# Another order of work at the entry to a gated MLP: six first-half product pairs ahead, sums begun before the norm

## The chip, the cores and the metric

One core of one Trainium2 chip runs the whole program. The time is the device time in microseconds (us) of one execution. The engines of the core are TensorE (PE, with its weight loads shown apart as PEld), VectorE (DVE), ScalarE (ACT), GpSimd (POOL) and SyncE (SP), which here only starts DMA transfers.

## The reference, cut to what matters

One layer of a trunk over 1024 tokens of 1024 features, in fp32:

```python
mod = silu(c) @ ada_w + ada_b                    # 6 x 1024 values
sh1, sc1, g1, sh2, sc2, g2 = split(mod, 6)
h = modulate(rmsnorm(x), sh1, sc1)               # mixers: pooling and gated linear attention
y = concat([y_pool, y_gla]) @ w_out
x = x + g1 * y
h = modulate(rmsnorm(x), sh2, sc2)               # the MLP begins here
up = h @ w_up                                    # 1024 -> 2 x 2816
y = causal depthwise conv (width 3) of up, + conv_b
a, b = split(y, 2)
x = x + g2 * ((silu(a) * b) @ w_down)
return rmsnorm(x) * final_norm
```

`modulate(h, shift, scale)` is `h * (1 + scale) + shift`. The change lies at the line `h = modulate(rmsnorm(x), sh2, sc2)` and the first products of `h @ w_up`.

## The kernel before, in words

Activations lie feature by feature: a tile holds 128 features of 512 tokens, so there are two token halves (0 and 1) of eight tiles each. Every fp32 factor of a product is split into a rounded high part and the remainder (`wsplit`, `split_b`, `mod_split`: a cast on ACT, a subtraction on DVE), and each product is three matmuls (`mm3`: high by high, low by high, high by low).

The MLP's up-projection multiplies a 2x2 block of weights (two halves of the input features) with a 2x2 block of activations (two token halves) with seven products in place of eight, in the Strassen-Winograd manner. The seven kinds, for each of 22 output blocks i, are products of sums of weight blocks with sums of activation blocks. In the code (1, i) and (2, i) multiply blocks of token half 0 alone. Kinds 5, 6, 3, 7 and 4 need half 1: their activation operands `ops_a` are made by `norm2_second` from the eight tiles `x1[1]` of half 1, the eight normalised tiles `x1[0]` of half 0, and the row scale `r` of half 1. One product of one kind for one block is 12 matmuls (four tiles by three).

`order` is the list of products. The first RAMP = 3 blocks are a ramp: (1, i) and (2, i) of these come first, and (5, i), which needs half 1, follows; from block 3 on all seven kinds of a block stand together. `up_step` gives out one product: it accumulates in a PSUM bank, ACT copies results out (`sp`, `ca`, `u`) or back in as the start of another accumulation (`seeded`, tile `upy`; where the bank is among the first eight, one small matmul with `prime` or `w` goes ahead of the copy), DVE adds, and ACT and DVE do the convolution (`conv`). `up_weight` loads a 512 KB tile of `w_up` (tile `ua`, from the `raw` pool of four buffers), forms the weight sums on DVE and splits them into a buffer that `slot()` hands out (names `ws` and `xs`). `prepare(n)` does this ahead of need: LOOK = 4 products ahead.

Ahead of the MLP stand the mixers' projections (`r`, then `u` jobs), then `jobs_out(0)` and `jobs_out(1)`, the output projection for half 0 and half 1: eight jobs each, each with its own 512 KB tile of `w_out` (also in the `raw` pool), split into the `wh` and `wl` buffers, two of each. `evac` adds the gated result to x (L693, DVE), stores it, squares it on ACT, and POOL adds the squares (`nsa`); `rstd_of` sums over the features by a matmul with ones (`ss`) and takes the root with two ACT instructions (`nr`). The conditioning vector `mod` is made beside all this, one tile `ada` of 512 KB at a time (`mod_tile`, L216 and L219), again through the `raw` pool: `run_jobs(jobs, mods_each)` does `mods_each` such tiles after each job, 32 in all.

PE executes in the order in which the program gives it. On ACT, DVE, POOL and in SP's queue a planner moves instructions by its own estimates, and each then executes strictly in the order that it set.

Of the kernel before, what the change touches and what calls it, by code (L numbers as in the profile page):

```python
# [28 lines left out]
P = 128  # L29
NK = 8  # L30
S = 1024
T = 512
# [21 lines left out]
def trunk_kernel(ctx, tc, xT, cvec, adaT, vecs, w_start, w_z, w_qkru, w_v, w_g2, w_pool,  # L54
# [612 lines left out]
    def jobs_out(hf):  # L667
# [24 lines left out]
        def evac(d, pp):  # L692
            dve.scalar_tensor_tensor(out=x1[hf][d], in0=pp, scalar=modv[:, 16 + d:17 + d],  # L693
                                     in1=x1[hf][d], op0=ALU.mult, op1=ALU.add)
            nc.sync.dma_start(out=x1d[hf][d], in_=x1[hf][d])
            own = s2 if hf else None
            if d == 0:
                nacc[hf] = s2(name="nsa") if hf else tmp("nsa")
            nacc[hf] = sumsq_step(nacc[hf], d, x1[hf][d], pool_e, True, own)
        return [mk(i) for i in range(8)]  # L700

    nacc = {}
    x1d = [[tc.dram_tile([P, T], F32, name=f"x1d{hf}{d}") for d in range(NK)] for hf in range(2)]
    gd = [tc.dram_tile([P, S], F32, name=f"gd{m}") for m in range(NFF)]
# [56 lines left out]
    for names, mods_each in (("k0 z q0 k1 v0 v1 v2 v3 q1", 0), ("r0 r1 r2 r3", 2),  # L761
                             ("u0 u1 u2 u3", 1)):
        run_jobs([named[i] for i in names.split()], mods_each)
# [14 lines left out]
    def slot():  # L778
        tag = ("wh", "xs", "wl", "xs")[slot_n[0] % 4]
        slot_n[0] += 1  # L780
        if tag == "xs":
            t = xs_pool.tile([P, 2, 4, P], F32R, tag="xs", name="xs")
        else:
            t = wp.tile([P, 2, 4, P], F32R, tag=tag, name="ws")
        return t[:, 0], t[:, 1]
# [43 lines left out]

    RAMP = 3  # L830
    order = [(n, i) for i in range(RAMP) for n in (1, 2)]
    for i in range(NFF):
# [12 lines left out]

    prepare(2)
    run_jobs(late[5:], 1)
    php.close()
# [17 lines left out]
    def small(name):  # L866
        return up_pool.tile([P, T], F32, tag="u", name=name, bufs=6)

# [3 lines left out]
    def norm2_second():  # L872
        r = rstd_of(nacc[1], s2)
        shs = const.tile([P, 4], F32, name="shs")
        dve.tensor_tensor(out=shs, in0=modv[:, 24:28], in1=modv[:, 28:32], op=ALU.add)

        def a22(name, dt=F32):
            return up_pool.tile([P, T], dt, tag="a22", name=name, bufs=10)

        def split_b(t, bias, mk):  # L880
            h, l = mk(dt=F32R, name="sh"), mk(dt=F32R, name="sl")
            if bias is None:
                act.copy(out=h, in_=t)
                sub(dve, l, t, h.bitcast(F32))
            else:
                act.activation(out=h, in_=t, func=AF.Identity, bias=bias, scale=1.0)  # L886
                dve.scalar_tensor_tensor(out=l, in0=t, scalar=bias, in1=h.bitcast(F32),  # L887
                                         op0=ALU.add, op1=ALU.subtract)
            return h, l

        t0, t1 = x1
        sums = []
        for k in range(4):
            for kk in (k, k + 4):
                mod_head(t1[kk], t1[kk], r, 32, kk)
            s = a22("s1")
            dve.tensor_tensor(out=s, in0=t1[k], in1=t1[k + 4], op=ALU.add)
            ops_a[5][k] = split_b(s, shs[:, k:k + 1], s2)
            sums.append(s)
        for k in range(4):  # L900
            sub(pool_e, t1[k], t0[k], t1[k])
            sub(dve, sums[k], sums[k], t0[k])
            ops_a[6][k] = split_b(sums[k], modv[:, 28 + k:29 + k], s2)
        for k in range(4):
            sub(pool_e, t0[k + 4], t0[k + 4], sums[k])
            ops_a[3][k] = split_b(t0[k + 4], None, s2)
            ops_a[7][k] = split_b(t1[k], None, s2 if k < 3 else a22)
        for k in range(4):
            ops_a[4][k] = split_b(t1[k + 4], modv[:, 28 + k:29 + k], a22)

# [20 lines left out]

    def seeded(src, w):
        primed = banks[0] >= 8
        y = bank("upy")
        if not primed:
            mm(y, w[0][:, 0], ops_a[1][0][0], True, True)
        act.copy(out=y, in_=src)  # L937
        return y

    def up_step(kind, i):  # L940
        w = weights.pop((kind, i))
        u = st_u.setdefault(i, {})
        where = {1: "x", 2: "x", 5: "z", 3: "z", 6: "y", 7: "y", 4: "y"}[kind]
        if kind in (1, 5):
            u[where] = bank("up" + where)
        elif kind == 6 and i < RAMP:
            u["y"] = seeded(u["s"], w)
        pp = u[where]
        product(pp, w, ops_a[kind], kind not in (1, 5))
        if kind == 1:  # L950
# [3 lines left out]
            else:  # L954
                u["y"] = seeded(pp, w)
        elif kind == 2:
            u["ca"] = cy("ca")
            act.copy(out=u["ca"][:, 0:T], in_=pp)
        elif kind in (5, 6):
            u[kind] = small("u")  # L960
# [25 lines left out]
    prepare(6)  # L986
    LOOK = 4
    for n, (kind, i) in enumerate(order[:-1]):
        prepare(n + 1 + LOOK)
        up_step(kind, i)  # L990
        if n == 1:
            norm2_second()

# [284 lines left out]
```

## Time and profile before

| what | value |
|---|---|
| median of three runs | 1082.6 us (1080.9 to 1084.25) |
| the profiled execution | 1082.63 us, its span on the core 1080.9 us |
| mean granted TensorE clock | 0.977 |
| PE busy | 1021.6 us (95%), 4480 matmuls |
| DVE busy | 856.0 us (79%) |
| ACT busy | 546.2 us (51%) |
| POOL busy | 200.1 us (19%) |
| DMA | 152.64 MB, 141 GB/s on the mean |

The profile's page shows busy shares of the span in 40 slices of 27 us; the chain of waits follows the last instruction back to what released it; the timeline gives single instructions with, in square brackets, how long the engine had been idle before and what ended that. The entry to the MLP lies between 344 us (the end of the output projection for half 0) and 456 us.

### The profile page before, as it was taken

Reading aid. Unit: us, or ns where it says so; the run is one execution under the profiler, and the core shown is the slowest. Engines: PE = TensorE matmul, PEld = TensorE weight load, DVE = VectorE, ACT = ScalarE, POOL = GpSimd, SP = SyncE. Lnnn points to the kernel's source line nnn. Section 1 sums busy time; section 2 is a strip of 40 time slices with the busy share of each in tenths; the row PEclk is TensorE's granted clock in tenths of the full one; section 3 lists DMA queues with packets and bytes.
Section 4 is the critical chain, followed back from the end, with each engine's and each line's share of the span. In section 5 each row is a group of like instructions: output and inputs, shape, how many; then the busy total and the mean of one; then the engine's idle time right before and its main releaser. Section 6 shows DMA issues by size and latency. Waiting matters only on the chain.

```text
span 1080.9 us, 12664 instructions
## 1 busy us (share of the span) xinstructions
PE 1021.6 (95%) x4480; PEld 816.2 (76%) x4480; DVE 856.0 (79%) x1189; ACT 546.2 (51%) x881; POOL 200.1 (19%) x171
## 2 busy tenths in 40 slices
PE   6989999999898986899999999999999999999986
PEld 4668878887786764688888888888888888888875
DVE  7967999688897959997776777767767686988884
ACT  5475484534534435655554555545545544644542
POOL 3436203131132115011011010010110100200210
PEclk8999999999899998999999999999999999999998
DMA  8743331454577530232223223322233895323542
GB/s 311 256 137 106 98 112 64 148 184 136 166 262 253 202 129 20 78 117 98 88 89 117 88 98 108 108 107 98 106 127 111 294 328 193 98 98 98 187 154 78
DMA packets 60385, 152.64 MB, mean 141 GB/s; under 512 B 6593, under 2 KB 9761, under 8 KB 60322
## 3 DMA queue, kind: packets, MB, share of 16 engines
q1 hardware_dynamic: 53760, 132.43, 36.2%
q0 software_dynamic: 4928, 17.30, 4.1%
q10 hardware_dynamic: 1634, 2.10, 0.6%
q8 instruction: 35, 0.57, 0.2%
q14 instruction: 28, 0.23, 0.1%
HBM read 126.12 MB, written 25.69 MB: 140 GB/s over the span
## 4 chain that ended last, share of the span: by engine, by line
PE 74%; DVE 16%; DMA 3%; ACT 3%; issue 3%; POOL 1%; SPq 0%; POOLq 0%; ACTq 0%; DVEq 0%
PE dn L107 18%; PE upy L107 17%; PE pp L107 14%; PE upz L107 11%; PE upx L107 10%; DVE wl L153 2%; PE sc L107 1%; DVE ada L219 1%; DVE hl L275 1%; DMA ada<-in_adaT_dram 1%; PE ss L107 1%; DVE la L376 1%; DMA da<-in_w_down_dram 1%; DVE sl L887 1%; DVE x L267 1%
## 5 line engine op out<-in xcount | busy, mean ns | idle before, releaser
L107 PE MATMUL dn<-ws,xs 128*128 128x512 f32 (+1 forms) x936 | 212.9, 389 | 2.8 <-DVE xs L1087 2.8
L107 PEld LDWEIGHTS dn<-ws,xs 128*128 128x128 f32 x936 | 175.3, 189 | 40.0 <-issue 3.7
L107 PE MATMUL upy<-sh,xs 128*128 128x512 f32 x272 | 92.2, 400 | 6.1 <-ACT upy L937 6.1
L107 PE MATMUL upy<-sh,ws 128*128 128x512 f32 x256 | 85.7, 395 | 0.9 <-ACT upy L937 0.9
L975 POOL DMA_DIRECT2D gd<-y x22 | 12.0, 545 | 372.6 <-DVE y L974 372.6
L793 DVE TENSOR_TENSOR xs<-ua,xs 128x512 fp32r<-128x512 f32 x77 | 54.8, 711 | 31.4 <-ACT xs L792 31.4
L153 DVE TENSOR_TENSOR wl<-raw,wh 128x1024 fp32r<-128x1024 f32 (+1 forms) x50 | 63.5, 1270 | 17.2 <-ACT wh L152 17.0
L107 PE MATMUL pp<-hl,wh 128*128 128x512 f32 x176 | 70.9, 403 | 5.4 <-DVE hl L275 5.4
L107 PE MATMUL pp<-hh,wh 128*128 128x512 f32 x176 | 73.9, 420 | 1.0 <-ACT hh L274 1.0
L792 ACT CAST xs<-ua 128x512 fp32r<-128x512 f32 x77 | 47.9, 622 | 52.1 <-PE upy L107 21.4
L107 PE MATMUL pp<-hh,wl 128*128 128x512 f32 x176 | 70.8, 402 | 2.3 <-DVE wl L153 2.3
L793 DVE TENSOR_TENSOR ws<-ua,ws 128x512 fp32r<-128x512 f32 x77 | 54.2, 704 | 22.1 <-ACT ws L792 22.1
L792 ACT CAST ws<-ua 128x512 fp32r<-128x512 f32 x77 | 48.0, 623 | 42.1 <-PE upy L107 20.6
L792 ACT CAST ws<-da 128x512 fp32r<-128x512 f32 x58 | 36.1, 622 | 63.9 <-PE dn L107 47.7
L107 PEld LDWEIGHTS upy<-sh,xs 128*128 128x128 f32 x272 | 51.8, 190 | 19.5 <-ACT upy L937 6.8
L803 DVE TENSOR_TENSOR ua<-ua 128x512 f32<-128x512 f32 x88 | 62.7, 713 | 2.2
L107 PE MATMUL upz<-sh,ws 128*128 128x512 f32 x184 | 62.2, 397 | 1.7 <-ACT sh L886 1.7
L152 ACT CAST wh<-raw 128x1024 fp32r<-128x1024 f32 (+1 forms) x50 | 50.4, 1008 | 24.1 <-PE pp L107 7.8
L107 PE MATMUL pp<-yh,wh 128*128 128x512 f32 x128 | 55.5, 434 | 6.7 <-ACT us L515 3.5
L107 PE MATMUL upx<-hh,xs 128*128 128x512 f32 x176 | 59.1, 397 | 2.4 <-ACT sp L953 2.4
L107 PE MATMUL upx<-hh,ws 128*128 128x512 f32 x176 | 59.3, 398 | 0.2 <-DVE x L693 0.2
L347 POOL TENSOR_TENSOR le<-b 128x512 f32<-128x512 f32 x24 | 33.7, 1406 | 137.7 <-PE dg L107 52.4
(252 smaller groups left out, 2461.1 us busy)
## 6 DMA issues: line engine op xcount, KB each, us to landing
ua<-in_w_up_dram SPq DMA_DIRECT2D x46, 512.0 KB, 3.3
ada<-in_adaT_dram SPq DMA_DIRECT2D x32, 512.0 KB, 3.8
gd<-y POOLq DMA_DIRECT2D x22, 512.0 KB, 2.9
raw<-in_w_qkru_dram SPq DMA_DIRECT2D x18, 512.0 KB, 3.5
da<-gd SPq DMA_DIRECT2D x36, 256.0 KB, 2.8
da<-in_w_down_dram SPq DMA_DIRECT2D x36, 256.0 KB, 3.4
raw<-in_w_out_dram SPq DMA_DIRECT2D x16, 512.0 KB, 4.3
x<-in_xT_dram SPq DMA_DIRECT2D x24, 256.0 KB, 4.5
```

The source lines that it names most:

```text
L107: pe.matmul(out=out, lhsT=lhsT, rhs=rhs, start=start, stop=stop, skip_group_check=more)
L152: act.copy(out=wh, in_=raw)
L153: dve.tensor_tensor(out=wl, in0=raw, in1=wh.bitcast(F32), op=ALU.subtract)
L219: dve.scalar_tensor_tensor(out=a, in0=a, scalar=1.0, in1=cb, op0=ALU.mult, op1=ALU.mult, accum_out=acc)
L267: dve.scalar_tensor_tensor(out=t, in0=x, scalar=modv[:, sc_c + k:sc_c + k + 1], in1=r, op0=ALU.mult, op1=ALU.mult)
L275: mark["split"] = dve.scalar_tensor_tensor(out=l, in0=t, scalar=sh, in1=h.bitcast(F32), op0=ALU.add, op1=ALU.subtract)
L347: pool_e.tensor_tensor(out=e.rearrange("p (n h) -> p n h", n=nb), in0=b.rearrange("p (n h) -> p n h", n=nb), in1=bb[:, :, 0, h - 1:h].broa ...
L376: dve.copy_predicated(out=av.rearrange("p a (n two h) -> p a n two h", two=2, h=h)[:, :, :, 1], mask=cit[:, mi].rearrange("p (n h) -> p n ...
L792: act.copy(out=h, in_=src)
L793: dve.tensor_tensor(out=l, in0=src, in1=h.bitcast(F32), op=ALU.subtract)
L803: eng.tensor_tensor(out=out, in0=a, in1=b, op=ALU.subtract)
L975: nc.gpsimd.dma_start(out=gd[i], in_=ya)
```

## The change

It does six things.

1. RAMP is 6: the first twelve products of the MLP are kinds 1 and 2 of six blocks, in the order (1,0) (1,1) (2,0) (1,2) (2,1) ... (1,5) (2,4) (2,5). The sum of squares `ss` of half 1 stands after the first of these, not after the second.
2. `evac` of half 1 begins the sums of kind 5 before the row scale is known: ACT multiplies tiles 0 to 3 by their scale in place, DVE adds tile k+4 times its scale. `norm2_second` then multiplies these four sums by `r`.
3. `norm2_second` is a generator in pieces, of which two are given out after each product. Its operands come in the order 5, 6, 3, 4, 7. Eight subtractions that POOL did are gone or on DVE.
4. For the ramp blocks the copy that starts `upy` stands at kind 5, not at kind 6, the copies of kind 2's result stand at kind 5 of the blocks, and the small matmul ahead is done for blocks 0, 1 and 2.
5. `slot()` hands out four `xs` buffers and then the `wh` and `wl` ones. `prepare(4)` stands ahead of the last three jobs of `jobs_out(1)` in place of `prepare(2)`.
6. The `u` jobs do two `ada` tiles each, not one; with that all 32 are done before `jobs_out(1)`, which before did the last four.

```diff
+            if hf and d >= 4:
+                sums[d - 4] = up_pool.tile([P, T], F32, tag="a22", name="s1", bufs=10)
+                dve.scalar_tensor_tensor(out=sums[d - 4], in0=x1[1][d],
+                                         scalar=modv[:, 32 + d:33 + d], in1=x1[1][d - 4],
+                                         op0=ALU.mult, op1=ALU.add)
             own = s2 if hf else None
...
             nacc[hf] = sumsq_step(nacc[hf], d, x1[hf][d], pool_e, True, own)
+            if hf and d < 4:
+                act.mul(out=x1[1][d], in_=x1[1][d], mul=modv[:, 32 + d:33 + d])
...
-                             ("u0 u1 u2 u3", 1)):
+                             ("u0 u1 u2 u3", 2)):
...
-        tag = ("wh", "xs", "wl", "xs")[slot_n[0] % 4]
+        tag = ("xs", "xs", "xs", "xs", "wh", "wl", "wh", "wl")[slot_n[0] % 8]
...
-    RAMP = 3
-    order = [(n, i) for i in range(RAMP) for n in (1, 2)]
+    RAMP = 6
+    order = [(1, 0)]
+    for i in range(RAMP):
+        order += [(1, i + 1)] if i + 1 < RAMP else []
+        order.append((2, i))
...
-    prepare(2)
-    run_jobs(late[5:], 1)
+    prepare(4)
+    run_jobs(late[5:])
...
         t0, t1 = x1
-        sums = []
         for k in range(4):
-            for kk in (k, k + 4):
-                mod_head(t1[kk], t1[kk], r, 32, kk)
-            s = a22("s1")
-            dve.tensor_tensor(out=s, in0=t1[k], in1=t1[k + 4], op=ALU.add)
-            ops_a[5][k] = split_b(s, shs[:, k:k + 1], s2)
-            sums.append(s)
+            dve.tensor_tensor(out=sums[k], in0=sums[k], in1=r, op=ALU.mult)
+            ops_a[5][k] = split_b(sums[k], shs[:, k:k + 1], s2)
+            yield
         for k in range(4):
-            sub(pool_e, t1[k], t0[k], t1[k])
             sub(dve, sums[k], sums[k], t0[k])
             ops_a[6][k] = split_b(sums[k], modv[:, 28 + k:29 + k], s2)
+            yield
         for k in range(4):
-            sub(pool_e, t0[k + 4], t0[k + 4], sums[k])
+            sub(dve, t0[k + 4], t0[k + 4], sums[k])
             ops_a[3][k] = split_b(t0[k + 4], None, s2)
-            ops_a[7][k] = split_b(t1[k], None, s2 if k < 3 else a22)
+            yield
         for k in range(4):
-            ops_a[4][k] = split_b(t1[k + 4], modv[:, 28 + k:29 + k], a22)
+            mod_head(t1[k + 4], t1[k + 4], r, 32, k + 4)
+            ops_a[4][k] = split_b(t1[k + 4], modv[:, 28 + k:29 + k], a22 if k < 3 else s2)
+            yield
+        for k in range(4):
+            sub(dve, sums[k], t1[k + 4], sums[k])
+            ops_a[7][k] = split_b(sums[k], None, s2)
+            yield
...
+    RAMP_COPIES = ((0, 1), (2,), (3,), (4, 5))
...
+        if kind == 5 and i < RAMP:
+            for n in RAMP_COPIES[i] if i < len(RAMP_COPIES) else ():
+                st_u[n]["ca"] = cy("ca")
+                act.copy(out=st_u[n]["ca"][:, 0:T], in_=st_u[n].pop("x"))
         if kind in (1, 5):
             u[where] = bank("up" + where)
-        elif kind == 6 and i < RAMP:
-            u["y"] = seeded(u["s"], w)
+        if kind == 5 and i < RAMP:
+            u["y"] = seeded(u["s"], w[0][:, 0] if i < 3 else None)
...
+    second = norm2_second()
     for n, (kind, i) in enumerate(order[:-1]):
         prepare(n + 1 + LOOK)
         up_step(kind, i)
-        if n == 1:
-            norm2_second()
+        for _ in range(2):
+            next(second, None)
```

Line numbers in the rows of the changed program are its own: its L802, L812, L899 and L906 are what `wsplit`, `sub`, `split_b` and the product with `r` issue, L698 is the sum in `evac`.

**DVE, from the last evacuation on.** `x_33..` are the last four tiles of half 1, `s_..` the sums of kind 5, `nr` the row scale, `ua` with `ws` or `xs` a weight tile and its split. Before:

```order
L693 SCALAR_TENSOR_TENSOR x_3324<-pp,modv,x_3324 128x512
L793 TENSOR_TENSOR ws<-ua,ws 128x512
L803 TENSOR_TENSOR ua<-ua 128x512 x2
L793 TENSOR_TENSOR ws<-ua,ws 128x512
L803 TENSOR_TENSOR ua<-ua 128x512 x2
L793 TENSOR_TENSOR xs<-ua,xs 128x512
L793 TENSOR_TENSOR ws<-ua,ws 128x512
L803 TENSOR_TENSOR ua<-ua 128x512 x2
L793 TENSOR_TENSOR xs<-ua,xs 128x512
L267 SCALAR_TENSOR_TENSOR x_3107<-x_3107,modv,nr 128x512
L267 SCALAR_TENSOR_TENSOR x_3318<-x_3318,modv,nr 128x512
```

In the changed program:

```order
L693 SCALAR_TENSOR_TENSOR x_3334<-pp,modv,x_3334 128x512
L698 SCALAR_TENSOR_TENSOR s_3381<-x_3332,modv,x_3117 128x512
L698 SCALAR_TENSOR_TENSOR s_3391<-x_3334,modv,x_3119 128x512
L693 SCALAR_TENSOR_TENSOR x_3336<-pp,modv,x_3336 128x512
L693 SCALAR_TENSOR_TENSOR x_3338<-pp,modv,x_3338 128x512
L698 SCALAR_TENSOR_TENSOR s_3401<-x_3336,modv,x_3121 128x512
L698 SCALAR_TENSOR_TENSOR s_3411<-x_3338,modv,x_3123 128x512
L802 TENSOR_TENSOR ws<-ua,ws 128x512 x3
L802 TENSOR_TENSOR xs<-ua,xs 128x512
L906 TENSOR_TENSOR s_3381<-s_3381,nr 128x512
L906 TENSOR_TENSOR s_3391<-s_3391,nr 128x512
```

Four sums came in among the evacuations, the weight sums (`ua<-ua`) of kinds 5 and 6 left this place, and the first use of `nr` is the product with a finished sum.

**SP's queue, from the last stores of half 0 on.** `x1d` are stores of x, `raw` the tiles of `w_out`, `ua` those of `w_up`. Before:

```order
L695 DMA x1d_603<-x_2864 128x512
L216 DMA ada<-in_adaT_dram 128x1024
L158 DMA raw<-in_w_out_dram 128x1024
L216 DMA ada<-in_adaT_dram 128x1024
L800 DMA ua<-in_w_up_dram 128x1024
L158 DMA raw<-in_w_out_dram 128x1024
```

In the changed program:

```order
L158 DMA raw<-in_w_out_dram 128x1024 x5
L695 DMA x1d_600<-x_2878 128x512
L695 DMA x1d_601<-x_2880 128x512
L695 DMA x1d_602<-x_2882 128x512
L695 DMA x1d_603<-x_2884 128x512
L809 DMA ua<-in_w_up_dram 128x1024 x3
```

The `ada` loads left this stretch, the loads of the five first `w_out` tiles stand together ahead of it, and three `w_up` tiles are loaded where one was, ahead of the last three `w_out` tiles.

**PE, at the first product of kind 5 and the first of kind 6.** Before, the small matmul `upy<-hh` stands between them:

```order
L107 MATMUL upz<-sl,ws 128x512
L107 MATMUL upz<-sh,ws 128x512
L107 MATMUL upy<-hh,xs 128x512
L107 MATMUL upy<-sh,xs 128x512
L107 MATMUL upy<-sl,xs 128x512
```

In the changed program it stands ahead of both:

```order
L107 MATMUL upx<-hl,xs 128x512
L107 MATMUL upx<-hh,xs 128x512
L107 MATMUL upy<-hh,ws 128x512
L107 MATMUL upz<-sh,ws 128x512
L107 MATMUL upz<-sl,ws 128x512
```

The copy that starts `upy` follows this small matmul on ACT, so twelve matmuls of kind 5 now stand between it and the first matmul of kind 6.

More of the change, by code (lines that the diff above doesn't have):

```diff
@@ L699, in evac @@
             nacc[hf] = sumsq_step(nacc[hf], d, x1[hf][d], pool_e, True, own)
+            if hf and d < 4:
+                act.mul(out=x1[1][d], in_=x1[1][d], mul=modv[:, 32 + d:33 + d])
         return [mk(i) for i in range(8)]
     nacc = {}
+    sums = [None] * 4
+    up_pool = None
     x1d = [[tc.dram_tile([P, T], F32, name=f"x1d{hf}{d}") for d in range(NK)] for hf in range(2)]
@@ L866, in small @@
     def small(name):
-        return up_pool.tile([P, T], F32, tag="u", name=name, bufs=6)
+        return up_pool.tile([P, T], F32, tag="u", name=name, bufs=7)
     ops_a = {1: hs[0][0:4], 2: hs[0][4:8], 3: [None] * 4, 4: [None] * 4, 5: [None] * 4,
@@ L873, in norm2_second @@
         r = rstd_of(nacc[1], s2)
-        shs = const.tile([P, 4], F32, name="shs")
+        shs = modv[:, 24:28]
         dve.tensor_tensor(out=shs, in0=modv[:, 24:28], in1=modv[:, 28:32], op=ALU.add)
@@ L889, in split_b @@
             return h, l
+        yield
         t0, t1 = x1
-        sums = []
         for k in range(4):
-            for kk in (k, k + 4):
-                mod_head(t1[kk], t1[kk], r, 32, kk)
-            s = a22("s1")
-            dve.tensor_tensor(out=s, in0=t1[k], in1=t1[k + 4], op=ALU.add)
-            ops_a[5][k] = split_b(s, shs[:, k:k + 1], s2)
-            sums.append(s)
+            dve.tensor_tensor(out=sums[k], in0=sums[k], in1=r, op=ALU.mult)
+            ops_a[5][k] = split_b(sums[k], shs[:, k:k + 1], s2)
+            yield
         for k in range(4):
-            sub(pool_e, t1[k], t0[k], t1[k])
             sub(dve, sums[k], sums[k], t0[k])
             ops_a[6][k] = split_b(sums[k], modv[:, 28 + k:29 + k], s2)
+            yield
         for k in range(4):
-            sub(pool_e, t0[k + 4], t0[k + 4], sums[k])
+            sub(dve, t0[k + 4], t0[k + 4], sums[k])
             ops_a[3][k] = split_b(t0[k + 4], None, s2)
-            ops_a[7][k] = split_b(t1[k], None, s2 if k < 3 else a22)
+            yield
         for k in range(4):
-            ops_a[4][k] = split_b(t1[k + 4], modv[:, 28 + k:29 + k], a22)
+            mod_head(t1[k + 4], t1[k + 4], r, 32, k + 4)
[4 more added lines that the diff above has]
+            ops_a[7][k] = split_b(sums[k], None, s2)
+            yield
     def product(out, w, a, more):
@@ L930, in add_to, with seeded @@
         return out
-    def seeded(src, w):
-        primed = banks[0] >= 8
+    def seeded(src, prime):
         y = bank("upy")
-        if not primed:
-            mm(y, w[0][:, 0], ops_a[1][0][0], True, True)
+        if prime is not None:
+            mm(y, prime, ops_a[1][0][0], True, True)
         act.copy(out=y, in_=src)
         return y
+    RAMP_COPIES = ((0, 1), (2,), (3,), (4, 5))
     def up_step(kind, i):
@@ L954, in up_step @@
             else:
-                u["y"] = seeded(pp, w)
-        elif kind == 2:
+                u["y"] = seeded(pp, None)
+        elif kind == 2 and i >= RAMP:
             u["ca"] = cy("ca")
             act.copy(out=u["ca"][:, 0:T], in_=pp)
+        elif kind == 2:
+            pass
         elif kind in (5, 6):
```

## The prediction

> **What bounds the kernel now.** I read the page first: its totals, then its 40 slices.
>
> ```profile
> PE 1021.6 (95%) x4480; PEld 816.2 (76%) x4480; DVE 856.0 (79%) x1189; ACT 546.2 (51%) x881; POOL 200.1 (19%) x171
> PE   6989999999898986899999999999999999999986
> ```
>
> PE is the bound, and its weakest slice outside the two ends is number 16 of 40, 405 to 432 us. So the second view is the stretches around it (columns: length, then PE, PEld, DVE, ACT, POOL busy, granted clock, DMA share, GB/s).
>
> ```profile
> 374.20:397.24 23.04, 18.56 (x73) 13.03 (x72) 8.87 (x10) 5.95 (x8) 1.20 (x2) 1.00 0.35 123
> 397.24:455.46 58.22, 43.26 (x163) 31.41 (x163) 55.85 (x70) 31.99 (x54) 17.71 (x11) 0.88 0.17 60
> 459.50:473.70 14.20, 14.20 (x63) 11.40 (x62) 13.55 (x16) 8.61 (x13) 2.59 (x3) 1.00 0.30 94
> 407.78:442.80 35.02, 22.30 (x79) 15.70 (x78) 35.02 (x43) 18.66 (x32) 13.64 (x8) 0.81 0.09 31
> 500.00:848.00 348.00, 348.00 (x1493) 279.54 (x1492) 255.06 (x315) 179.01 (x266) 43.63 (x54) 1.00 0.30 106
> ```
>
> From 500 us on PE never rests. At the entry it lacks work, DVE does not rest from the arrival of the row scale (407.78) to 442.80, and the granted clock is 0.81 there. The third view, the waits of PE from 397 to 456 us, names what was late; the fourth is the chain.
>
> ```profile
> PE upy L107 <- ACT upy L937: 7.1, 2, 6.1
> PE upz L107 <- DVE sl L887: 2.7, 1, 2.7
> PE upx L107 <- ACT sp L953: 2.4, 3, 1.1
> PE upz L107 <- ACT sh L886: 1.7, 1, 1.7
> ```
>
> ```profile
> 404.64 1.73 PE ss L107 x4
> 847.62 2.75 PE dn L107 x12
> 850.37 2.80 PE upy L107 x12
> ```
>
> One product is 2.80 us. From 397.24, the end of the output projection, to 853.17, the end of the last row, behind which only the down-projection follows, stand 154 products (431.2), one of the down-projection (2.75), the two `ss` matmuls, 1.3 by their starts in the timeline below (404.48 to the next start, 405.79), and two small ones (0.5): 435.7 of 455.9. **So 20.2 us are there to be had**, in waits and in matmuls at a slow clock, all before 456 us.
>
> **The change, part by part.**
>
> *The longer ramp.* Six more products that need only half 0 stand behind `ss`: eleven in place of four, 30.8 us against 11.2. In that time DVE has to make the operands. These are its prices, and POOL's part in them:
>
> ```profile
> 418.30 1.78 DVE L803 TENSOR_TENSOR s<-s,x 128x512 f32<-128x512 f32 x1
> 428.65 0.68 DVE L803 TENSOR_TENSOR s<-s,x 128x512 f32<-128x512 f32 x1
> 417.79 1.74 POOL L803 TENSOR_TENSOR x<-x,x 128x512 f32<-128x512 f32 x1 [1.89 <-DVE s L897]
> L803 POOL TENSOR_TENSOR x<-x,s 128x512 f32<-128x512 f32 x4 | 6.8, 1715 | 2.5 <-DVE s L803 2.5
> ```
>
> The same subtraction takes 1.78 us while a subtraction of POOL runs (417.79 to 419.53) and 0.68 without. The eight on POOL are gone. DVE gets four sums ahead of the norm and, behind it, 20 remainders, 20 products or subtractions, and by DVE's order 10 weight splits or sums up to the last operand of kind 7: 50 by about 0.63 (the 0.68 row less its overlap with the next), 31.5 us. By the parts below the output projection ends at 392.5, POOL's sums at 398.0, `ss` at 399.7, and `r` comes 1.4 later (407.78 against the end of the `ss` row above, 406.37): 401.1. The last operand is then there at 432.6; PE comes to (5,0) at 431 to 432 and to (7,0), which needs that operand, 8.4 later. Kind 5's four operands need the first 10 of the 50. So the waits of the second list go; ACT's copy into `upy` (6.1 alone) now has the twelve matmuls of kind 5 over it, 2.8 us. If this cover failed, ACT's queue in between would cost again up to 6.1.
>
> *What stays of the wait.* `ss` now has one product ahead of it, and POOL's three last sums end where they ended.
>
> ```profile
> 396.74 4.74 POOL L234 TENSOR_TENSOR nsa<-nsa,nsq 128x512 f32<-128x512 f32 x3 [21.84 <-ACT nsq L230]
> 401.59 0.50 PE L107 MATMUL upx<-hh,xs 128*128 128x512 f32 x1 [1.09 <-ACT sp L953]
> 404.48 1.02 PE L107 MATMUL ss<-nsa,ones 128*128 128x512 f32 x2
> 405.79 0.80 PE L107 MATMUL upx<-hh,ws 128*128 128x512 f32 x1
> ```
>
> They end 4.24 us after PE's last output product (401.48 against 397.24). The first MLP product covers 3.0 of that. DVE's two inserted sums don't delay POOL, which needs 1.58 for each sum and is behind anyway. But in ACT's new order a weight split stands ahead of the first square and waits for a tile whose load begins only when the last `w_out` tile is split: about 1.3 more. So PE waits 2.5 (from 1.2, without that, to 4). A wait of this size has a price of its own at half 0's norm, which is the same pattern:
>
> ```profile
> 344.48 1.12 PE L107 MATMUL ss<-nsa,ones 128*128 128x512 f32 x2 [2.62 <-POOL nsa L234]
> 348.29 0.63 PE L107 MATMUL pp<-yh,wh 128*128 128x512 f32 x1
> 348.71 0.52 PE L107 MATMUL pp<-yl,wh 128*128 128x512 f32 x1
> 349.07 0.40 PE L107 MATMUL pp<-yh,wl 128*128 128x512 f32 x1
> ```
>
> After 2.62 us of rest the matmuls start 0.43 apart, not 0.23: from 344.48 to 349.07 stand the pair and five matmuls, 2.5 at full pace, 4.6 here, so 2.1 lost. After 1.09 (401.59) nothing was lost. I take 2.1, with 0 and 2.1 as ends. The Trainium skill ("TensorE: Matmul & The Clock Gate", Part 1) says that the clock falls to half after an idle window of about 3.4 us. By that 2.5 us would cost no clock and the time would be 2.1 lower; the row of 2.62 differs, so the row decides.
>
> One more small matmul costs 0.2. For short waits inside the ramp I put 1.0 (0 to 8). **Sum of this part: 20.2 - 2.5 - 2.1 - 0.2 - 1.0 = 14.4 gained.**
>
> *The last three output jobs.* Each is 24 matmuls, 5.6 us; three are 16.8 of the 23.04 in the first of the stretches. PE waited there for the splits:
>
> ```profile
> PE pp L107 <- ACT wh L152: 2.8, 3, 1.0
> PE pp L107 <- DVE wl L153: 1.6, 3, 0.6
> 376.61 4.76 DMA ua<-in_w_up_dram
> 381.92 1.05 ACT wh L152
> 383.00 1.24 DVE wl L153
> ```
>
> `(1,0)`'s split sat in one of two `wh` buffers, so a split could begin only when the job before had ended. Now both are free; but three `ua` tiles hold three of the four `raw` buffers, and the last three `w_out` tiles pass through the fourth one after the other: load 4.76 (the chain's row, a tile of the same size), cast 1.05, remainder 1.24, with gaps 7.1 a tile. The first is in time, the next two come 1.4 late each: 16.8 + 2.8 + 0.2 = 19.8. **Gain 3.2** (0 if the load takes 6, 6 if it takes 3.3, the page's median for `ua`).
>
> *The `ada` tiles.* One leaves the place ahead of half 0's last evacuations:
>
> ```profile
> 335.15 0.39 PE L107 MATMUL pp<-yh,wl 128*128 128x512 f32 x1
> 335.62 1.23 DVE L219 SCALAR_TENSOR_TENSOR ada<-ada,cb 128x1024 f32<-128x1024 f32 x1 [0.99 <-DMA ada<-in_adaT_dram]
> 337.08 2.73 DVE L693 SCALAR_TENSOR_TENSOR x<-pp,modv,x 128x512 f32<-128x512 f32 x4
> ```
>
> Its wait and work are 2.4 us, from 334.6 to 337.08 with the small instruction behind it; PE has the first of these results at 335.5 (the first row), so 1.5 can be had, and PE's wait of 2.62 at 344.48 shrinks by it. **Gain 1.5** (0 to 4.7, with its clock). The other three left a stretch where PE was busy. All four come into the `u` jobs, where DVE has this much room:
>
> ```profile
> 230.00:245.00 15.00, 14.18 (x74) 11.61 (x72) 12.79 (x19) 4.00 (x7) 4.00 (x3) 1.00 0.42 136
> 245.00:260.00 15.00, 12.87 (x65) 10.49 (x64) 12.71 (x21) 4.91 (x10) 5.28 (x3) 1.00 0.41 137
> 260.00:275.00 15.00, 14.70 (x60) 10.58 (x58) 12.55 (x23) 7.41 (x12) 0.00 (x0) 1.00 0.52 175
> 278.26 0.79 PE L107 MATMUL pp<-yh,wh 128*128 128x512 f32 x1 [3.51 <-ACT us L515]
> ```
>
> DVE is idle for 6.9 of 45 us; four tiles need 4 by 1.37 (1.23 and a small one), 5.5. PE's wait that ends this stage, 3.51 for ACT's copy `us`, follows DVE's chain; that copy now stands ahead of ACT's table load of 1.28, not behind it. I put **0** (a loss of 18 to a gain of 3).
>
> The sum is 14.4 + 3.2 + 1.5 + 0 = 19.1: a span of 1061.8 in place of 1080.9. What lies around the span was 1.7 in the profiled execution, 1082.63, which is the median; so **1063.5 us**.
>
> **The rivals.**
>
> *The `ada` tiles are paid in full.* In the `u` jobs two loads stand openly on the chain:
>
> ```profile
> 260.44 3.17 DMA ada<-in_adaT_dram
> 264.90 3.29 DMA ada<-in_adaT_dram
> ```
>
> A tile starts loading only when a `raw` buffer is free, so each of four new ones may cost load and work, 4.6: 18 us, and PE is full from 290 to 335, so it is passed on. About half of it gives 1072; all, 1082. For it: these rows. Against: DVE's 6.9 idle us and the copy's new place.
>
> *The ramp is fed too slowly.* Two products of the ramp, 5.6 us, need one tile, and a tile that waits for its buffer takes 7.1. Were the twelve fed through one buffer, they would last 9 longer: 1072. Against: when the last `w_out` tile is split, two buffers turn.
>
> *Slower: DVE and ACT set the pace of the six ramp blocks.* Kinds 5, 6, 3, 7, 4 of a block are 14.0 us of PE, and in 459.50:473.70 DVE was busy for 13.55 of 14.20. From 500 us on it is idle for 5.2 in 19.6. If that idleness is not slack but time in which DVE and ACT wait for each other, a block needs about 17.9, six blocks 23 more: 1086.5. It decides from 17.2 a block on. Against: two ramp blocks ran before without a wait of PE in that very stretch.
>
> *No change.* The sums are ready earlier but the waits come back as others of the same size. PE would have to lose some 19 us that no row shows: 1081.
>
> *More.* `ss` without its wait, full clock, loads of 3.3: 4.6 and 2.8 more, 1056.
>
> **How the numbers follow.** The forecast with its own terms (1057 to 1068) gets 0.64; the two that halve the gain (1068 to 1079) 0.18 together; more 0.08; no change 0.04; slower 0.06. The range 1056 to 1074 leaves out the upper half of the second and the last two. 0.3% is 3.2 us, about what this kernel's runs can tell from nothing: faster 0.90, the same 0.04, slower 0.06.
>
> **What would show it.** In the changed profile: PE without a wait above 0.7 us between `ss` and the first product of kind 4; `nr` done before (1,1) ends and one wait at `ss` of 1.2 to 4 us for POOL; three output jobs at the end of about 20 us; DVE subtractions of 0.68 throughout, no POOL work between the last `nsa` and the first store of `gd`; PE's wait in the first job of `jobs_out(0)` no longer than 3.5; blocks 0 to 5 at 14.0 us each. Wrong if the first MLP product starts later than 397, if (7,0) waits for DVE, or if a ramp block takes over 15 us.

## The result and the profile after

The changed kernel takes 1049.74 us (median of four runs, 1047.94 to 1052.67) against 1083.21 for the kernel before: ratio 0.9703, 95% interval 0.9684 to 0.9723. The gain is 33.5 us where 19.1 were forecast, and the time lies outside the range of 1056 to 1074.

The page of the changed kernel, busy time and slices:

```profile
span 1046.2 us, 12684 instructions
PE 1001.2 (96%) x4481; PEld 815.4 (78%) x4481; DVE 854.6 (82%) x1197; ACT 549.2 (52%) x888; POOL 190.5 (18%) x163
PE   7989999998999989999999999999999999999995
```

The hole in the sixteenth slice is closed, as intended. But PE is busy for 20.4 us less (1021.6 before) with one matmul more. Waits that are taken away don't shorten busy time; matmuls at full clock in place of a slow one do, but the entry accounts for 5.5 us of it (163 matmuls took 43.26 us from 397.24 to 455.46 before, and 37.73 from 389.27 to 427.00 after). The stretches say where the rest is (columns as in the prediction: length, busy time of PE, PEld, DVE, ACT and POOL with counts, granted clock, DMA share, GB/s). Before:

```profile
500.00:800.00 300.00, 300.00 (x1287) 240.99 (x1286) 223.36 (x276) 155.38 (x231) 36.34 (x45) 1.00 0.28 102
```

After:

```profile
374.70:386.79 12.09, 11.56 (x48) 8.77 (x48) 5.13 (x6) 3.41 (x5) 0.45 (x1) 1.00 0.42 142
386.79:389.27 2.48, 0.00 (x1) 0.01 (x1) 2.48 (x4) 1.17 (x3) 2.40 (x2) 1.00 0.42 155
389.27:427.00 37.73, 37.73 (x163) 30.55 (x164) 36.92 (x58) 24.49 (x42) 2.01 (x2) 1.00 0.21 70
500.00:800.00 300.00, 300.00 (x1326) 248.39 (x1325) 234.25 (x285) 160.16 (x237) 38.61 (x48) 1.00 0.30 107
```

In 300 us in which PE rests in neither kernel, at a granted clock of 1.00 in both, the changed one does 1326 matmuls and the one before 1287: 3% more. This is far behind the last operand of the entry, in a stretch where the diff changes only which buffers `slot()` hands out. The chain of waits shows it product by product, before and after:

```profile
508.82 2.80 PE upz L107 x12
511.62 2.80 PE upy L107 x12
```

```profile
509.07 2.72 PE upy L107 x12
511.79 2.72 PE upz L107 x12
813.71 2.73 PE upy L107 x12
```

A product takes 2.72 us in place of 2.80. The waits of PE in the changed kernel from 386 to 500 us are these two, and at the first MLP product its new wait of 2.48 us costs no clock:

```profile
PE upx L107 <- DVE x L693: 2.5, 1, 2.5
PE upy L107 <- DVE cb L944: 2.1, 2, 1.2
```

```profile
389.27 0.50 PE L107 MATMUL upx<-hh,xs 128*128 128x512 f32 x1 [2.48 <-DVE x L693]
389.60 0.40 PE L107 MATMUL upx<-hl,xs 128*128 128x512 f32 x1
```

So there are two questions: what the new order is worth by itself, and why all products are quicker.

### The profile page after: what moved, and what is told of

The parts are those of the page before. It is cut to its first block, busy times and chain, and to the rows that moved or that the text cites. A ratio compares the mean times of both kernels' runs of the same rounds, so it can differ in the third digit from the quotient of the medians.

```text
span 1046.2 us, 12684 instructions
## 1 busy us (share of the span) xinstructions
PE 1001.2 (96%) x4481; PEld 815.4 (78%) x4481; DVE 854.6 (82%) x1197; ACT 549.2 (52%) x888; POOL 190.5 (18%) x163
## 4 chain that ended last, share of the span: by engine, by line
PE 62%; DVE 23%; DMA 5%; ACT 4%; issue 4%; POOL 2%; SPq 0%; POOLq 0%; ACTq 0%; DVEq 0%
PE dn L107 18%; PE upy L107 14%; PE upx L107 9%; PE upz L107 9%; PE pp L107 8%; DVE wl L153 3%; DVE ada L219 2%; DMA ada<-in_adaT_dram 2%; DVE xs L802 2%; DVE hl L275 2%; POOL le L347 1%; DVE la L376 1%; DVE ua L812 1%; DVE lq L359 1%; PE ss L107 1%
## 5 line engine op out<-in xcount | busy, mean ns | idle before, releaser
L107 PE MATMUL dn<-xs 128*128 128x512 f32 (+1 forms) x480 | 111.1, 386 | 1.7 <-DVE xs L802 1.3
L107 PE MATMUL dn<-ws 128*128 128x512 f32 x456 | 108.3, 394 | 2.3 <-DVE xs L1110 2.3
L107 PEld LDWEIGHTS dn<-xs 128*128 128x128 f32 x480 | 88.5, 188 | 21.1 <-DVE xs L802 2.1
L107 PEld LDWEIGHTS dn<-ws 128*128 128x128 f32 x456 | 86.7, 190 | 20.9 <-issue 2.7
L107 PE MATMUL upy<-sh,xs 128*128 128x512 f32 x264 | 86.6, 390 | 2.1 <-DVE cb L944 2.1
L802 DVE TENSOR_TENSOR xs<-ua,xs 128x512 fp32r<-128x512 f32 x78 | 60.6, 782 | 14.8 <-ACT xs L801 14.8
L802 DVE TENSOR_TENSOR ws<-ua,ws 128x512 fp32r<-128x512 f32 x76 | 55.1, 727 | 15.7 <-ACT ws L801 15.7
L107 PE MATMUL upx<-hh,xs 128*128 128x512 f32 x192 | 62.8, 392 | 2.5 <-DVE x L693 2.5
L812 DVE TENSOR_TENSOR ua<-ua 128x512 f32<-128x512 f32 x88 | 60.2, 687 | 2.1 <-DMA ua<-in_w_up_dram 0.3
L347 POOL TENSOR_TENSOR le<-b 128x512 f32<-128x512 f32 x24 | 37.1, 1549 | 134.1 <-DVE lq L359 53.8
L937 DVE SCALAR_TENSOR_TENSOR y<-ca,vec,y 128x1023 f32<-128x1023 f32 (+1 forms) x44 | 56.3, 1280 | 4.3 <-ACT y L934 3.5
```

The source lines that it names most:

```text
L107: pe.matmul(out=out, lhsT=lhsT, rhs=rhs, start=start, stop=stop, skip_group_check=more)
L347: pool_e.tensor_tensor(out=e.rearrange("p (n h) -> p n h", n=nb), in0=b.rearrange("p (n h) -> p n h", n=nb), in1=bb[:, :, 0, h - 1:h].broa ...
L802: dve.tensor_tensor(out=l, in0=src, in1=h.bitcast(F32), op=ALU.subtract)
L812: eng.tensor_tensor(out=out, in0=a, in1=b, op=ALU.subtract)
L937: dve.scalar_tensor_tensor(out=y[:, sh:], in0=c[:, :S - sh], scalar=cw[j], in1=y[:, sh:], op0=ALU.mult, op1=ALU.add)
```

## The experiments

**Where the quicker products come from.** The part of the change on the shift sums has one line that the diff above leaves out:

```diff
-        shs = const.tile([P, 4], F32, name="shs")
+        shs = modv[:, 24:28]
```

The sums stand in `modv` now, and a constant tile of 16 bytes, which takes 32 in SBUF, is gone. Constants are allocated first from the left, so every left-side tile, among them all activations, starts 32 bytes lower; weights are allocated from the right and stay. The built programs give the addresses. Difference of the two starts, moving operand less weights, modulo 256 bytes, over the products of 512 columns:

```
before    32: 2850   0:  912   224: 192   others:  37
after      0: 3915  32:   40              others:  37
```

In the MLP's up-projection it is 32 for every product before and 0 for every product after. That the matmuls' pace followed this was theory A; theory B was that PE keeps a better pace because it no longer stalls on its way in. Three kernels tell them apart, two of them the kernel before with nothing but placement changed.

`a1_free` is the kernel before with the two lines above.

> The kernel before with one edit: the four shift sums of the entry stand in columns 24 to 27 of modv and not in a constant tile of their own (16 bytes, which takes 32 in SBUF). No instruction is added, removed or moved; every tile that is allocated from the left starts 32 bytes lower. In the program 2997 products of the kernel before read a moving operand that starts at 0 of 64 bytes and weights at 32 of 64, and 960 read both at 32; here 4081 read both at 32. Theory A (placement: a product of 128x128 by 128x512 starts the next one 6.5 ns later where the two start at different remainders of 64 bytes): a product of twelve takes 2.72 us and not 2.80 in the MLP, and the time is 2997 x 6.5 ns = 19 us less, less some for stretches in which TensorE waits anyway: 1064 to 1068. Theory B (the shorter spacing came with the new order, because TensorE no longer stalls on its way into the MLP): 2.80 as before, 1080 to 1086.

Measured: 1070.71 us, 0.9906 (0.9883 to 0.9928) of the kernel before. The pace is that of the changed kernel, and PE's waits in the entry are those of the kernel before, to 0.2 us (the stretch first, then two of the waits from 386 to 456 us):

```profile
500.00:800.00 300.00, 300.00 (x1325) 248.48 (x1324) 232.90 (x284) 159.54 (x236) 38.64 (x48) 1.00 0.30 106
```

```profile
PE upy L107 <- ACT upy L937: 7.1, 2, 6.1
PE upz L107 <- DVE sl L887: 2.5, 1, 2.5
```

Theory B falls. The gain of 11.4 is less than expected (1064 to 1068), because ahead of the MLP nothing of it arrives: the first MLP product starts at 397.44 in both, and PE's waits for the splits of the output weights just ahead of it are the same (2.8 and 1.7 us, 2.8 and 1.6 before).

`b1_shift` is the changed kernel with the opposite shift:

```diff
-    epsb = const.tile([P, 1], F32, name="epsb")
+    two = const.tile([P, 2], F32, name="two")
+    epsb, oneb = two[:, 0:1], two[:, 1:2]
     dve.memset(epsb, EPS)
-    oneb = const.tile([P, 1], F32, name="oneb")
```

> The changed kernel with one edit: the two one-column constants of the norms share a tile, so that all that follows them from the left starts 32 bytes lower and the 2997 products read their operands at 0 and 32 of 64 bytes, as in the kernel before. Theory A: a product of twelve takes 2.80 us again in the MLP, the time is 1050 + 17 to 20 = 1067 to 1070, and the distance to the kernel before, 13 to 16 us, is what the new order itself is worth. Theory B: 2.72, 1048 to 1053.

Measured: 1062.1 us, 0.982 (0.9801 to 0.9838). The slow pace is back (difference 224 modulo 256 in the whole up-projection), with the new order in place:

```profile
500.00:800.00 300.00, 300.00 (x1288) 241.50 (x1287) 228.33 (x282) 156.76 (x232) 36.98 (x47) 1.00 0.30 105
```

This is the comparison that the prediction was about: at the old pace the new order is worth 20 us.

`d00` is the kernel before with both edits and an unused 32-byte tile at the right end, so that the weights move too:

```diff
+    padr = ctx.enter_context(tc.tile_pool(name="padr", bufs=1, side="right"))
+    padr.tile([P, 4], F32, name="pad")
     rawp = ctx.enter_context(tc.tile_pool(name="rawp", bufs=4, side="right"))
```

> The kernel before with three edits of placement alone: shift sums in modv, the two one-column constants in one tile, and an unused 32-byte tile at the right end of SBUF, so that the weights start 32 bytes lower too. 4036 products then read both operands at 0 of 64 bytes. If it is the two starts that must agree (theory A), it is as quick as with both at 32: 2.72 us for a product of twelve, 1064 to 1068. If the moving operand has to start at 32 of 64 (theory A2), it stays at 2.80 and 1080 to 1086, and so it does by theory B.

Measured: 1069.69 us, 0.9877 (0.9856 to 0.9898), 1325 matmuls in the 300 us. So it is the distance of the two operands that counts here, not where one of them starts.

**How the distance sets the pace.** Two kernels do nothing but products, PE alone at work, each measured in a single execution.

> None of the kernel's own work is done (the output is zeros): 26 groups of 48 products of 128x128 by 128x512 in fp32r, one behind the other, with nothing beside them on the other engines. Weights and moving operand start at a chosen distance from an address that is a multiple of 64 bytes: ga (moving 0, weights 0), gb (32, 0), gc (32, 32), gd (0, 32), ge to gq (4, 8, 16, 24, 28, 36, 40, 48, 56, 60, 64, 96, 128; weights 0), gr (0, 16), gs (0, 48), gt (16, 16), gu (48, 16), gv (16, 48), gw (moving 0 and 32 in turn, weights 0), gx (moving 0, weights 0 and 32 in turn), gy (both in turn), gz (0, 0) again. Theory A (the two starts must agree modulo 64 bytes): ga, gc, go, gq, gt and gz take 48 x 226.7 ns = 10.9 us, gb, gd, gp, gu and gv 48 x 233.3 = 11.2 us, and those in between tell how far from agreement it begins. Theory A3 (each operand by itself: a start that isn't a multiple of 64 costs): ga, go, gq quick, gc slow. Theory C (the price comes from VectorE and ScalarE reading the same memory beside TensorE): all groups alike.

The timeline, 48 products a row; the distance to the next row's start, divided by 48, is the pace:

```profile
21.52 11.04 PE L88 MATMUL ga<-mv,wt 128*128 128x512 f32 x48
32.40 11.37 PE L88 MATMUL gb<-mv,wt 128*128 128x512 f32 x48
43.60 11.07 PE L88 MATMUL gc<-mv,wt 128*128 128x512 f32 x48
...
177.10 11.15 PE L88 MATMUL go<-mv,wt 128*128 128x512 f32 x48
188.08 11.37 PE L88 MATMUL gp<-mv,wt 128*128 128x512 f32 x48
199.29 11.36 PE L88 MATMUL gq<-mv,wt 128*128 128x512 f32 x48
210.50 11.35 PE L88 MATMUL gr<-mv,wt 128*128 128x512 f32 x48
```

(moving 0, weights 0) takes 226.7 ns and (32, 0) 233.3, as in the kernel, but (128, 0) takes 233.5 and (64, 0) 228.8: the expectation by remainders of 64 bytes failed. The effect stands with nothing beside PE, so theory C falls too. Starts that aren't multiples of 32 bytes gave 226.9 to 236.7 without a rule that I could see ((28, 0) 226.9, (4, 0) 236.7, (16, 16) 230.0). A full grid on multiples of 32, where the allocator puts tiles, settled the rest.

> Again none of the kernel's own work (the output is zeros): 256 groups of 16 products of 128x128 by 128x512 in fp32r, with the moving operand at 0, 32, ... 480 bytes (second letter a to p) and the weights at 0, 32, ... 480 bytes (third letter a to p) from two starts that are multiples of 512 bytes apart. Weights stand 512 bytes apart within a group. In the run of 26 groups before it, equal remainders of 64 bytes weren't enough: weights at 0 with the moving operand at 128 took 11.21 us for 48, as at 32, where 0 took 10.88. In the kernel's programs the quick products have starts that differ by a multiple of 512 bytes and the slow ones by 32 bytes more or less than such a multiple. Theory A4 (the difference of the starts must be a multiple of 512): the 16 groups with equal letters take 3.63 us and all others 3.73. Theory A5 (a period shorter than 512): quick groups also at some fixed other differences. Theory A6 (not the difference but the pair): the map isn't the same along a diagonal.

The first rows of its timeline, 16 products each, weights at 0 and the moving operand at 0, 32, 64 and 96 (gaa to gda), and at 256 and 288 (gia, gja); the pace is the distance to the next row's start:

```profile
21.66 3.79 PE L85 MATMUL gaa<-mv,wt 128*128 128x512 f32 x16
25.28 3.90 PE L85 MATMUL gba<-mv,wt 128*128 128x512 f32 x16
29.02 3.83 PE L85 MATMUL gca<-mv,wt 128*128 128x512 f32 x16
32.69 3.89 PE L85 MATMUL gda<-mv,wt 128*128 128x512 f32 x16
...
51.34 3.79 PE L85 MATMUL gia<-mv,wt 128*128 128x512 f32 x16
54.98 3.90 PE L85 MATMUL gja<-mv,wt 128*128 128x512 f32 x16
```

3.62, 3.74, 3.67, then 3.64 again at 256. Over all 256 pairs, from the starts of the products in the trace, by moving less weights:

```
difference modulo 256 bytes     ns a product (lowest and highest of its 32 pairs)
  0                             227.4 (226.7 to 228.4)
 64                             229.6 (228.8 to 229.7)
 32, 96, 128, 160, 192, 224     232.8 to 234.2 by difference (232.3 to 234.3)
```

Theory A5 holds: the pattern repeats after 256 bytes and runs along the diagonals. Why, inside the chip, no run shows.

**What the parts of the new order are worth**, each undone in the changed kernel at its quick pace. The differences below are between medians of different sessions, in which the kernel before itself took 1081.4 to 1083.2 us, so differences of a microsecond or two are not resolved.

`c1_ada`:

```diff
-                             ("u0 u1 u2 u3", 2)):
+                             ("u0 u1 u2 u3", 1)):
...
-    run_jobs(late[5:])
+    run_jobs(late[5:], 1)
```

> The changed kernel with the modulation tiles (ada) spread as before: one behind each of u0 to u3 of half 1 and one behind each of the last three output jobs, so that two stand in the jobs of half 0's output again. If these two were what held up half 0's evictions on VectorE (the wait for us of 3.51 us at 278.26 and the one at the norm's reduction of 2.62 us at 344.48 in the kernel before, each followed by products at half rate, against 2.34 and 0.87 with no half rate after the change), the first reduction comes 3 to 4 us later, at 343.5 to 344.5, and the time is 1052 to 1055. If they cost the 1.5 us of the prediction: 1051 to 1052. If nothing: 1048 to 1051.

Measured: 1060.09 us, 0.9797 (0.977 to 0.9824), 10 more than the changed kernel and far over every expectation. The first reduction comes 2.4 later (342.89 against 340.48). The larger part lies in the last three output jobs. DVE's and PE's timeline:

```profile
370.37 3.56 DVE L802 TENSOR_TENSOR xs<-ua,xs 128x512 fp32r<-128x512 f32 x4
373.86 2.28 DVE L153 TENSOR_TENSOR wl<-raw,wh 128x1024 fp32r<-128x1024 f32 x1
```

```profile
376.19 0.80 PE L107 MATMUL pp<-yh,wl 128*128 128x512 f32 x1 [3.49 <-DVE wl L153]
376.79 0.63 PE L107 MATMUL pp<-yh,wh 128*128 128x512 f32 x1
377.21 0.63 PE L107 MATMUL pp<-yl,wh 128*128 128x512 f32 x1
```

An `ada` tile stands in the way there (DVE works on it at 361.1, and the load of the next `w_up` tile begins only at 362.3, by the chain), so four weight splits of the MLP come late and together, ahead of the remainder `wl` that PE waits for; after these 3.49 us the matmuls start 0.42 apart, up to 381.5. From the first reduction to the first MLP product that makes 54.5 us against 48.8.

`c2_slots`:

```diff
-        tag = ("xs", "xs", "xs", "xs", "wh", "wl", "wh", "wl")[slot_n[0] % 8]
+        tag = ("wh", "xs", "wl", "xs")[slot_n[0] % 4]
...
-    prepare(4)
+    prepare(2)
```

> The changed kernel with the weight slots of the MLP handed out in the old order (wh, xs, wl, xs) and two of the MLP's weight pairs made ahead of the last output jobs, not four: the first pair takes one of the buffers through which the output weights go, again. By the prediction's term the last three output jobs take 7.1 us each again and end 3.2 us later; of this the 2.48 us for which the first MLP product waits for the evictions are not won back, since those move along: 1052 to 1054. If the wait for evictions hides part of it, 1050 to 1051.

Measured: 1054.94 us, 0.9748 (0.9721 to 0.9776), 5.2 more. A little over the expectation. The two waits of the kernel before are back (its rows: 2.8 and 1.6), and the wait for the evictions stays:

```profile
PE pp L107 <- ACT wh L152: 2.7, 3, 0.9
PE upx L107 <- DVE x L693: 2.5, 1, 2.5
PE pp L107 <- DVE wl L153: 1.6, 3, 0.5
```

From the first reduction to the first MLP product it is 52.5 against 48.8: 3.7 for a term of 3.2. The rest is 0.8 earlier in the program and waits in the ramp.

`c12_ada_slots` has both edits.

> The changed kernel with both edits of the last two experiments: modulation tiles spread as before, and slots and first weight pairs as before. What is left of the change is the six pairs, the early sums and the placement. If the 7.4 us that the output weights then set for each of the last three jobs hide the modulation tiles on VectorE (as I took it for the kernel before), the two edits do not add up: 5 us for the slots and 2.5 us for the later evictions of half 0, 1056 to 1059. If they add up (10.4 and 5.2 us): 1063 to 1067.

Measured: 1061.29 us, 0.9792 (0.976 to 0.9824), between the two expectations: 11.6 over the changed kernel, where the single edits cost 10.4 and 5.2. They overlap: with the old slots `ada` costs 6.4, and with `ada` back in place the old slots cost 1.2, which these runs can't tell from nothing. What is left, the six pairs, the early sums and the new order of operands and copies (parts 1 to 4 of the change), follows against `a1_free`, which has the same pace: 1070.7 - 1061.3, about 9 us by the medians and 12 by the ratios.

`c3_three_pairs`:

```diff
-    RAMP = 6
+    RAMP = 3
...
-    RAMP_COPIES = ((0, 1), (2,), (3,), (4, 5))
+    RAMP_COPIES = ((0, 1), (2,))
...
-        for _ in range(2):
+        for _ in range(3):
```

> The changed kernel with three pairs ahead instead of six (three pieces of the norm per product, so that each stands in the program ahead of its use). The cover of the norm is then 6 x 2.72 = 16.3 us, the first product of kind 5 comes at about 407 and the first of kind 7 at 415, where the last operand of kind 7 is finished at 425.9 after the change. If VectorE's chain of operands is what the six pairs hide, TensorE waits 7 to 11 us there and the time is 1056 to 1061. If three pairs were enough (VectorE has fewer weight differences to make by then), 1048 to 1052.

Measured: 1056.17 us, 0.9759 (0.9736 to 0.9782), 6.4 more, at the low end of the first theory. The place is as expected, the size of the wait is not: PE waits 2.6 us at the first product of kind 7, not 7 to 11, and a slow clock follows (0.42 between matmuls). Waits and slow matmuls together cost 6.4 us there. The waits from 386 to 456 us, besides the one of 2.5 ahead of the MLP:

```profile
PE upy L107 <- ACT sh L895: 1.6, 1, 1.6
PE upy L107 <- DVE sl L812: 1.0, 2, 0.7
```

**The new wait of 2.48 us.** `e7_sums_late` puts the four sums behind all four evictions, with the reduction one product later:

```diff
-            if hf and d >= 4:
-                sums[d - 4] = ...
+            if hf and d == 7:
+                for e in range(4, 8):
+                    sums[e - 4] = ...
...
-        for _ in range(2):
+        for _ in range(2 if n else 0):
```

> The changed kernel with the four activation sums of the last output job behind all four of its evictions on VectorE, and the reduction of the norm (with all pieces behind it) one product later. If the 2.48 us before the first MLP product are the evictions held up behind the sums, that wait is gone and the first product starts at 386.8 to 387.3; the pieces then come at the times they come now. If TensorE sets the pace through the ramp the time is 2.0 to 2.5 us less, 1047 to 1048; if VectorE does (it is busy 98.6 of the 100 us from 400 to 500), the products of the ramp wait for it by as much and the time stays at 1049 to 1051.

Measured: 1051.9 us, 0.9721 (0.9706 to 0.9735). The wait shrinks to 0.2, so it was the evictions behind the sums. The time is no less: PE loses 6.9 us against its pace in the up-projection, where the changed kernel loses 3.8 (the stretch less 1867 steps of 226.7 ns). The work ahead of the MLP ended 3.9 us later in that profile besides (390.7 against 386.8), and the first product started at 390.9, not at 387 as expected, so a second test was made: `e10_free_bank` leaves VectorE's order as it is and gives the first product a PSUM bank that no eviction holds.

```diff
-            for n, nb in (("p", 4), ("s", 3), ("m", 1))}
+            for n, nb in (("s", 3), ("m", 1), ("p", 4))}
...
-        for _ in range(2):
+        for _ in range(2 if n else 0):
```

> The changed kernel with the PSUM pools laid out in another order, so that the first MLP product writes a bank that no eviction of the last output job holds, and with the norm's reduction (and all pieces behind it) one product later, which leaves it at about 392. VectorE has the same work in the same order. The 2.48 us before the first MLP product are then gone, it starts at 386.5 to 387. If TensorE sets the pace through the ramp: 2 to 2.5 us less than the changed kernel beside it. If VectorE does (98.6 of 100 us busy from 400 to 500), the products of the ramp wait for VectorE's sums by as much more, 2 to 2.5 us on top of the 2.4 at 465 and 480, and the time is that of the changed kernel within 1 us.

> The changed kernel as it is, beside the run with the free bank, on the same chip. By its first measurement 1048 to 1052.

Measured: 1051.25 us (0.9712, 0.9693 to 0.9731) with the free bank and 1050.33 (0.9706, 0.9683 to 0.9729) for the changed kernel beside it, the same within the noise. The wait is gone:

```profile
391.43 0.39 PE L107 MATMUL upx<-hh,xs 128*128 128x512 f32 x1
```

But the first product starts at 391.4, not at 386.5 to 387: as in `e7_sums_late`, the output projection ended later (391.6 against 387.4 in the run beside it), for a reason that is not shown. From 386 to 500 us PE has these waits in place of the one that went:

```profile
PE upy L107 <- DVE cb L944: 3.3, 4, 1.6
PE upx L107 <- ACT sp L973: 2.0, 1, 2.0
```

PE's time over its pace in the up-projection is 8.4 us against 5.5 in the run beside it. Counted from the end of the output projection, the matmul 600 places behind the first of the MLP starts 144.2 us later with the free bank and 144.0 without: what the missing wait saved came back inside the ramp, where PE is fed by VectorE and ScalarE (the rows above). That is one profile of each. Neither version beats the changed kernel.

## Why the prediction was wrong, by its own steps

**The step that failed is the count "154 products (431.2)" at 2.80 us a product.** It took the pace of a product as a constant of the kernel; the line that moved the shift sums into `modv` was priced at nothing. The pace fell to 2.72, which is 12.3 us on 154 products; by experiment the placement is worth 11.4 us in the kernel before and 12.4 in the changed one. With the old pace the new order takes 1062.1, 1.4 from the forecast of 1063.5 and in its range. Of the signs that I listed only "blocks 0 to 5 at 14.0 us each" has the pace in it, and only a block above 15 us was to count against the forecast; the first took 13.8 with its small matmul (424.02 to 437.85), 13.6 without.

The terms, in profiled spans, the kernel before against `b1_shift` (old pace) and the changed kernel. The last row ends at 853.17 in the kernel before, at 816.44 after (the row of 813.71 above) and at 832.20 in `b1_shift`, by its chain:

```profile
829.40 2.80 PE upy L107 x12
```

| from | before | `b1_shift` | after | forecast of the gain |
|---|---|---|---|---|
| start to first MLP product | 397.4 | 392.8 | 389.3 | 3.2 + 1.5 |
| to the end of the last row | 455.7 | 439.4 | 427.2 | 14.4 |
| to the end of the span | 227.7 | 227.7 | 229.7 | 0 |

- *The entry, 14.4:* 16.3 at the old pace. The 20.2 us that could be had were right: by the prediction's own sum of 435.7 the stretch of 455.7 has 20.0 to spare, and that of `b1_shift`, with one small matmul more, still has 3.5. Too much was taken off: the wait of 2.5 at `ss` for POOL didn't come, because the same 2.5 us came one product earlier, from VectorE, and lie outside this stretch. "DVE's two inserted sums don't delay POOL" was nearly right (POOL's last sum waits 0.40 us, and its sums end 4.9 us behind the last output product, where 5.5 were put). But they delay the evictions that PE waits for, and that wait was missed:

```profile
390.08 1.60 POOL L234 TENSOR_TENSOR nsa<-nsa,nsq 128x512 f32<-128x512 f32 x1 [0.40 <-ACT nsq L230]
```

- *The slow clock after a 2.5 us wait, 2.1:* 1.3 to 1.7 in five profiles with such a wait, next to nothing (0.1 to 0.2) in two, see the last section.
- *The cover:* VectorE's operands, put at 31.5 us, took 31.2 (395.45 to 426.6); PE came to (5,0) at 424.0 and found no wait at (7,0). Subtractions of 0.68 and the empty POOL came as foretold. With three pairs the wait of kind 7 is there (`c3_three_pairs`).
- *Short waits in the ramp, 1.0:* 1.5 in `b1_shift`, 2.8 after, with the slow matmuls behind them (456 to 500 us). The ramp is fed just fast enough; at the quicker pace a little less so.
- *The last three output jobs, 3.2:* 3.7 by `c2_slots`.
- *The `ada` tiles:* 1.5 for half 0's evictions, where 2.4 (`c1_ada`) to 3.5 (`b1_shift`) were measured, inside the 0 to 4.7. "The other three left a stretch where PE was busy", priced at nothing, was wrong for the new order: with `ada` put back (`c1_ada`), the stretch from the first reduction to the MLP is 5.7 longer. No loss came in the `u` jobs, as put. Forecast and `b1_shift` agree on 4.7 for the whole stretch before the MLP only because these gains and the new wait of 2.45 stand against each other.
- *Behind the last row:* 2.0 more after the change, put at nothing. PE has two new waits at the start of the down-projection, for the split of a weight tile:

```profile
PE dn L107 <- DVE xs L802: 1.3, 1, 1.3
PE dn L107 <- ACT xs L801: 0.4, 1, 0.4
```

  With the steps around them they cost 2.5 us. The first stands in `b1_shift` too (2.1 in all), and neither the kernel before nor `a1_free` has any, so they come with the new order; which part of it brings them no run shows. `b1_shift` takes no longer than the kernel before only because the last wait of the down-projection is shorter there (2.1 us against 2.8) and half pace followed it in the kernel before alone. `a1_free`, with neither the new waits nor half pace, takes 225.5.
- *The rivals:* neither of the two that halve the gain came, nor the slower one. "More" (1056) had the right side, but its causes, 4.6 and 2.8 us from waits, clock and loads, were not what made the difference.

## What to carry to other kernels

The price of a matmul taken from a trace holds for the addresses of that build. When an edit adds or drops any tile, also one of 16 bytes, compare the starts of moving operand and weights modulo 256 before pricing anything else, and look at the number of matmuls in a stretch without waits at a granted clock of 1.00. Then undo the placement alone, so that the order is judged at one pace. A wait taken away ahead of a stretch that other engines feed can come back inside it, as with the free bank.

## What the runs showed of the hardware that I had not expected

- Products of 128x128 by 128x512 start 227 to 234 ns apart by the distance of the starts of their two SBUF operands modulo 256 bytes, at a granted clock of 1.00 and with no other engine at work. The Trainium skill ("SBUF — State Buffer", Operand start alignment) asks that an operand start at a multiple of its element size and says that this is about legality, not speed; all 256 pairs of the grid obey it and differ by 3%.
- A wait of about 2.5 us costs clock or doesn't. The same wait ahead of the first MLP product was followed by full pace after the change (the row of 389.27 above) and by half pace in `b1_shift` (granted clock 0.50 from 392.78 to 394.20):

```profile
392.78 0.79 PE L107 MATMUL upx<-hh,xs 128*128 128x512 f32 x1 [2.45 <-DVE x L693]
393.38 0.63 PE L107 MATMUL upx<-hl,xs 128*128 128x512 f32 x1
393.80 1.05 PE L107 MATMUL upx<-hh,xs 128*128 128x512 f32 x2
```

  From this row to `ss` it took 2.88 us after the change and 2.86 in `c2_slots`, but 3.99 in the second profile of the changed kernel, 4.22 in `b1_shift`, and 4.27, 4.34 and 4.42 in `c1_ada`, `c3_three_pairs` and `c12_ada_slots`. The Trainium skill ("TensorE: Matmul & The Clock Gate", Part 1) calls the activity window free-running and its effect variable from run to run; these executions agree with that, and the prediction's fixed price for such a wait was too simple.
